# Splitting each expert weight piece into its high and low part with one instruction per engine instead of two

## The chip, the cores and the metric

The kernel runs on one core of a Trainium2 chip. The metric is the device time of one execution in microseconds (us). Engines are named as in the profile: PE is TensorE's matmul, PEld its weight load, DVE is VectorE, ACT is ScalarE, POOL is GpSimd, SP is the engine whose queue issues the weight DMAs. L174 is line 174 of the kernel before; the change adds three lines above the experts' code and one at its head, so L1209 before is L1213 after.

## The reference

Two layers of a decoder trunk over 256 tokens with model width 1024, all in float32. Each layer is a mixer (gated DeltaNet, convolution and attention heads between one input and one output projection) and a feed-forward part, each with a residual and a layer norm. The feed-forward part of layer 0 is dense; that of layer 1, which the change is about, sends each token to 2 of 8 experts of hidden width 3584:

```python
FFN_EXPERT = 7 * D_MODEL // 2          # 3584
logits = jnp.einsum('nd,de->ne', xf, w_router).astype(jnp.float32)
top_logits, top_idx = lax.top_k(logits, TOP_K)      # 2 of 8
gates = jax.nn.softmax(top_logits, axis=-1)
...
def expert_block(args):
    xb, e = args
    h = jax.nn.silu(xb @ w1[e]) * (xb @ w3[e])
    return h @ w2[e]
```

w1 and w3 are 1024 x 3584 and w2 is 3584 x 1024 for each expert. Every expert has tokens, so all 8 x 3 matrices are read, 352 MB.

## The kernel before

**Split products.** A float32 operand is split into a high part (type fp32r) and the low rest, and a product is the sum of three matmuls: high x high, high x low, low x high. `mm3` (L211) writes them: first, for each term, the two that use the weights' high part, and at the end of the group those that use the low part. `split` (L173) makes the two parts with one instruction each: ACT copies to the high part (L174), DVE subtracts it from the source (L175), so DVE's instruction waits for ACT's.

**A weight piece** is 128 partitions x 2048 columns of float32, 1 MB. `stage` (L177) issues its DMA on SP's queue into a tile `w`; `parts` (L189) allocates a tile `whi` and a tile `wlo` and splits the piece; `load` (L208) is the one after the other. Tiles come from two pools in turn, with 3 `w`, 2 `whi` and 2 `wlo` in each, so 6, 4 and 4 in all. `parts` splits in two halves of 128x1024, so a piece costs two instructions on ACT and two on DVE:

```python
        d = 2 if w.shape[1] == 2 else 1
        h = w.shape[d] // 2
        for c in (slice(0, h), slice(h, 2 * h)):
            c = (slice(None),) * d + (c,)
            split(w[c], *[t[c] for t in r])
        return r
```

A piece of w1 or w3 is cut by row blocks of the contraction (the first four of eight blocks, or the first two of four), a piece of w2 (two row blocks of 1024 columns) by columns, so that its first half feeds the output's columns 0 to 511 and the second half the columns 512 to 1023.

**The experts** (`moe`, L962) run after the router. Experts are ranked by their token count. `one_by_one` (L1195) takes four of them, each with up to 128 tokens, in 7 steps of 512 hidden columns: two pieces of w1, two of w3 (`first`, L1175), then the hidden tile h (Silu on ACT, L1208, product on DVE, L1209), then two pieces of w2 for the step before (`second`, L1184), then h is transposed on PE (L1218) and split into hT. That is 4 x 7 x 6 = 168 pieces. `side_by_side` (L1229) takes the largest expert, with up to 256 tokens, together with the three smallest of up to 64, in 14 steps of 256 hidden columns and a closing step: each step has one piece each of w1, w3 and w2 for the large one (matmuls at L215 to L224, hidden tile L1248 and L1249) and for each of the three small ones, whose matmuls are packed (`mm_packed`, L1164, matmuls at L1168 to L1172). That is another 14 x 12 = 168 pieces. `gather` (L1088) brings an expert's tokens together beforehand, `scatter` (L1127) adds its result to the residual; both come in small steps between the others. A branch for overfull experts (L1371) holds more pieces and is not executed with these inputs. The names in the rows: whi, wlo and w are a piece's tiles, x the gathered tokens, t a PSUM tile of the first layer, py one of the second layer, hT and jT the transposed hidden tile of a small and of the large expert.

**The order on each engine** is not written by hand: the framework's scheduler simulates a timeline (L1415) and issues each engine's instructions in the order that comes out. On PE it places the first matmul on a piece of w2 ahead of other work where that matmul's half is ready, and the rest of the piece later.

Of the kernel before, what the change touches and what calls it, by code (L numbers as in the profile page):

```python
# [38 lines left out]
def tile_hybrid_decoder(ctx: ExitStack, tc: tile.TileContext, x_in, w_in, mix_scale, w_out, gdn_conv_w,  # L39
# [7 lines left out]
    mixers = ctx.enter_context(ExitStack())  # L47
    mcst = mixers.enter_context(tc.tile_pool(name="mcst", bufs=1, reuse_waits="tile"))

    wp = {"more": None, "small": None, "n": 0,  # L50
          "base": ctx.enter_context(tc.tile_pool(name="wgt", bufs=1, side="right", reuse_waits="tile"))}


# [80 lines left out]
    par, small = [], []  # L134
# [38 lines left out]
    def split(src, hi, lo):  # L173
        S.activation(hi, src, AF.Copy)  # L174
        return V.tensor_sub(lo, src, hi.bitcast(F32))  # L175
# [13 lines left out]
    def parts(staged):  # L189

        which, w = staged
        r = []
        m = w.shape[1] * w.shape[2]
        for name, n in (("whi", WB[1]), ("wlo", WB[2])):
            if wp["small"] and m <= 1024:
                t = wp["small"].tile([128, 1024], F32R, name=name, tag=name, bufs=1)
            else:
                t = wp[which].tile([128, 2048], F32R, name=name, tag=name, bufs=n)
            r.append(t[:, :m].rearrange("p (a b) -> p a b", a=w.shape[1]))

        d = 2 if w.shape[1] == 2 else 1
        h = w.shape[d] // 2
# [5 lines that stand above are left out]
    def load(*args):  # L208
        return parts(stage(*args))
# [52 lines left out]
    def layer_norm_block(b, y, gam, bet, lp):  # L262

        xb = xt[:, b, :]
        r = lp.tile([128, D], F32, name="lnr", tag="lnr", bufs=2) if y else xb
        for h, yy in enumerate(y or ()):
            V.scalar_tensor_tensor(r[:, 512 * h:512 * h + 512], xb[:, 512 * h:512 * h + 512], ALPHA, yy,
                                   op0=OP.mult, op1=OP.add)
        st = lp.tile([128, 2, 6], F32, name="lnst", tag="lnst", bufs=2)
        for h in range(2):  # L270
            V.bn_stats(st[:, h, :], r[:, 512 * h:512 * h + 512])  # L271
        mv = lp.tile([128, 2], F32, name="lnmv", tag="lnmv", bufs=2)
        V.bn_aggr(mv, st)  # L273
        rs = lp.tile([128, 1], F32, name="lnrs", tag="lnrs", bufs=2)
        rsqrt_small(rs, mv[:, 1:2], 1, LN_EPS, 1.0, lp)
        for h in range(2):
            c = slice(512 * h, 512 * h + 512)
            V.scalar_tensor_tensor(r[:, c], r[:, c], mv[:, 0:1], gam[:, c], op0=OP.subtract, op1=OP.mult)  # L278
            last = V.scalar_tensor_tensor(xb[:, c], r[:, c], rs, bet[:, c], op0=OP.mult, op1=OP.add)  # L279
        return last  # L280
# [680 lines left out]

    def moe(l):  # L962
        li = l // 2
        with ExitStack() as es:
            gp = es.enter_context(tc.tile_pool(name="moe", bufs=1, reuse_waits="tile"))
            ps = es.enter_context(tc.tile_pool(name="eps", bufs=1, space=PSUM, reuse_waits="tile"))
# [41 lines left out]
            spare = [spare[0][:, :2048], spare[0][:, 2048:], gp.tile([128, 2048], F32, name="spare", tag="xg", bufs=2)]  # L1008
            early = [stage(*s, which=("more", "base")[i // 2]) for i, s in enumerate(piece_list[:4])]
            early[:2] = [parts(s) for s in early[:2]]  # L1010
            early += [stage(*s) for s in piece_list[4:10]]
            early += [stage(*s, into=t) for s, t in zip(piece_list[10:], spare)]

            def fetch(*src):
                nonlocal early
                if not early:
                    return load(*src)
                w = early.pop(0)
                return w if isinstance(w, list) else parts(w)
# [356 lines left out]
            n = None  # L1376
            for b in range(NB):
                with tc.issue_after(n.ins) if n else nullcontext():
                    n = layer_norm_block(b, None, gam, bta, gp)
# [8 lines left out]
    mixer(1)  # L1388
    mixers.close()
    moe(1)  # L1390


# [26 lines left out]
```

## Time and profile before

| | |
|---|---|
| median of 3 runs | 1656.45 us |
| lowest and highest | 1655.86 and 1656.79 us |
| the profiled execution | 1652.18 us |
| its span on the core | 1650.0 us |
| granted TensorE clock, mean | 0.983 |

The span is what the trace covers; the profiled execution is 2.18 us longer than its span, and 4.27 us shorter than the median of the runs. The experts' pieces are worked on from about 590 to about 1623 us; what is before are the first layer and the second mixer, what is behind is the last scatter and layer norm.

### The profile page before, as it was taken

What the parts mean: (1) busy time and instruction counts of PE and PEld (TensorE: products, weight loads), DVE (VectorE), ACT (ScalarE), POOL (GpSimd) and SP (SyncE); (2) the same over time, 40 slices, a digit from 0 to 9 for tenths busy, and PEclk for the clock granted to TensorE, in tenths of its full rate; (3) what the DMA queues carried; (4) which work ended last, traced back from release to release, by engine and by line L of the source; (5) the groups of instructions that cost most, each with busy time, mean ns of one, the idle gap of its engine ahead of it and who ended that gap; (6) DMA issues with size and microseconds to landing.
All of it is one profiled execution on the core that took longest, in us unless ns stands there. A gap on an engine that the chain in (4) does not pass through costs nothing. (4 is left out here: it accounts for less than half of the span.)

```text
span 1650.0 us, 28322 instructions
## 1 busy us (share of the span) xinstructions
PE 1573.9 (95%) x11218; PEld 1365.8 (83%) x11218; DVE 1369.6 (83%) x1902; ACT 1020.6 (62%) x1375; POOL 66.3 (4%) x82
## 2 busy tenths in 40 slices
PE   7999999999899989999999999999999999999995
PEld 6887799997888768888888888888988889888893
DVE  7987854555998798998988889887998988899997
ACT  5234544442425557777777677676887776777782
POOL 5001100000201100000000000000000000000000
PEclk9998999999999999999999999999999999999998
DMA  5351755532324577999999999998999989999991
GB/s 153 98 167 50 245 195 191 177 115 79 91 65 155 189 255 267 360 367 340 359 345 347 330 345 352 344 330 273 359 363 332 347 305 333 366 318 340 342 375 62
DMA packets 274796, 430.05 MB, mean 261 GB/s; under 512 B 11900, under 2 KB 181938, under 8 KB 274656
## 3 DMA queue, kind: packets, MB, share of 16 engines
q1 hardware_dynamic: 272864, 423.81, 74.8%
q0 software_dynamic: 1792, 4.35, 0.8%
q8 instruction: 90, 1.47, 0.4%
q14 instruction: 50, 0.41, 0.1%
HBM read 427.08 MB, written 1.05 MB: 259 GB/s over the span
## 5 line engine op out<-in xcount | busy, mean ns | idle before, releaser
L175 DVE TENSOR_TENSOR wlo<-w,whi 128x1024 fp32r<-128x1024 f32 (+1 forms) x812 | 939.1, 1204 | 135.2 <-ACT whi L174 127.5
L174 ACT ACTIVATE whi<-w 128x1024 fp32r<-128x1024 f32 (+1 forms) x812 | 792.1, 1037 | 231.3 <-PE py L217 43.3
L215 PE MATMUL t<-whi,x 128*128 128x512 f32 x448 | 179.4, 401 | 0.5 <-DVE x L175 0.5
L217 PE MATMUL t<-whi,x 128*128 128x512 f32 x448 | 176.1, 393 | 0.0
L222 PE MATMUL t<-wlo,x 128*128 128x512 f32 x448 | 124.5, 396 | 0.0
L215 PE MATMUL t<-x,whi 128*128 128x256 f32 x448 | 109.5, 282 | 0.0
L219 PE MATMUL t<-x,whi 128*128 128x256 f32 x448 | 109.4, 282 | 0.0
L215 PE MATMUL pj<-xth,whi 128*128 128x256 f32 x368 | 99.3, 303 | 6.6 <-ACT whi L174 2.5
L215 PEld LDWEIGHTS t<-whi,x 128*128 128x128 f32 x448 | 84.3, 188 | 20.1 <-DVE x L175 0.7
L222 PEld LDWEIGHTS t<-wlo,x 128*128 128x128 f32 x448 | 83.8, 188 | 20.1 <-DVE wlo L175 0.4
L217 PEld LDWEIGHTS t<-whi,x 128*128 128x128 f32 x448 | 84.4, 188 | 18.2
L219 PE MATMUL pj<-xtl,whi 128*128 128x256 f32 x368 | 95.7, 294 | 0.0
L1168 PE MATMUL t<-whi,x 128*128 128x256 f32 x588 | 86.9, 287 | 8.5 <-DVE x L175 3.3
L1170 PE MATMUL t<-wlo,x 128*64 128x256 f32 x672 | 93.8, 281 | 0.0
L1168 PEld LDWEIGHTS t<-whi,x 128*128 128x128 f32 x588 | 77.8, 190 | 14.6 <-DVE h L1249 4.4
L215 PE MATMUL py<-whi,hT 128*128 128x512 f32 x224 | 88.0, 393 | 0.0
L217 PE MATMUL py<-whi,hT 128*128 128x512 f32 x224 | 87.4, 390 | 0.0
L219 PE MATMUL ph<-xtl,whi 128*128 128x256 f32 x352 | 85.4, 281 | 0.4 <-DVE xtl L260 0.4
L215 PE MATMUL ph<-xth,whi 128*128 128x256 f32 x352 | 85.3, 281 | 0.0
L219 PEld LDWEIGHTS t<-x,whi 128*128 128x128 f32 x448 | 84.4, 188 | 0.8
L215 PEld LDWEIGHTS t<-x,whi 128*128 128x128 f32 x448 | 84.4, 188 | 0.8
L1170 PEld LDWEIGHTS t<-wlo,x 128*64 128x64 f32 x672 | 81.1, 135 | 1.8
(430 smaller groups left out, 2814.9 us busy)
## 6 DMA issues: line engine op xcount, KB each, us to landing
w<-in_moe_w_dram SPq DMA_DIRECT2D x333, 1024.0 KB, 6.2
w<-in_ffn_w_dram SPq DMA_DIRECT2D x33, 1024.0 KB, 5.5
w<-in_w_in_dram SPq DMA_DIRECT2D x18, 1024.0 KB, 5.6
w<-in_w_out_dram SPq DMA_DIRECT2D x8, 1024.0 KB, 5.0
w<-in_w_in_dram SPq DMA_DIRECT2D x14, 512.0 KB, 4.3
spare<-in_moe_w_dram SPq DMA_DIRECT2D x3, 1024.0 KB, 7.8
xt<-in_x_dram SPq DMA_DIRECT2D x2, 512.0 KB, 4.0
gam<-in_ln_mix_g_dram POOLq DMA_DIRECT2D x2, 512.0 KB, 3.9
```

What stands on the lines that cost most here:

```text
L174: S.activation(hi, src, AF.Copy)
L175: return V.tensor_sub(lo, src, hi.bitcast(F32))
L215: T.matmul(o, a[0], b[0], start=first and i == 0, stop=False)
L217: T.matmul(o, a[1], b[0], start=False, stop=False)
L219: T.matmul(o, a[0], b[1], start=False, stop=False)
L222: m = T.matmul(o, a[0], b[1], start=False, stop=last and i == n - 1)
L1168: T.matmul(o, flat(a), b[0], start=first and i == 0, stop=False)
L1170: T.matmul(o[:64], a[:, 0, :], b[1], start=False, stop=False)
```

## The change

A flag `whole` is false at first and set at the head of `moe`. With it, `parts` splits a piece with one ACT instruction and one DVE instruction of 128x2048. Tiles, DMAs and matmuls are those of before, and all code ahead of `moe` is as it was.

```diff
-    wp = {"more": None, "small": None, "n": 0,
+    wp = {"more": None, "small": None, "n": 0, "whole": False,
           "base": ctx.enter_context(tc.tile_pool(name="wgt", bufs=1, side="right", reuse_waits="tile"))}
...
             r.append(t[:, :m].rearrange("p (a b) -> p a b", a=w.shape[1]))
+        if wp["whole"]:
+            split(w, *r)
+            return r
 
         d = 2 if w.shape[1] == 2 else 1
...
     def moe(l):
         li = l // 2
+        wp["whole"] = True
```

The scheduler orders the program anew. The order on SP and on POOL is the same as before. On PE the number of matmuls is the same; ACT and DVE have one instruction less for each piece.

On ACT, at the first hidden tile of `one_by_one` (h is the Silu, hT the split of its transpose), before:

```order
331 L174 ACTIVATE whi<-w 128x1024 x4
332 L1208 ACT_TABLE_LOAD
333 L1208 ACTIVATE h<-t_6960 128x512
334 L174 ACTIVATE whi<-w 128x1024 x4
335 L174 ACTIVATE hT<-t_7013 128x512
```

and with the change:

```order
331 L174 ACTIVATE whi<-w 128x2048 x2
332 L1212 ACT_TABLE_LOAD
333 L1212 ACTIVATE h<-t_6952 128x512
334 L174 ACTIVATE whi<-w 128x2048 x2
335 L174 ACTIVATE hT<-t_7005 128x512
```

Four pairs of halves have become four whole copies, in the same places between the other instructions.

On DVE at the same place (by, posj and oh belong to the router's and the gather's small work, h is the product that PE's first transpose reads), before:

```order
771 L175 TENSOR_TENSOR wlo<-w,whi 128x1024 x2
772 L1349 TENSOR_REDUCE posj<-by 128x8
773 L175 TENSOR_TENSOR wlo<-w,whi 128x1024 x2
774 L1348 TENSOR_TENSOR by<-job,gate 128x64
775 L1101 TENSOR_SCALAR oh<-slots,posj 128x128 x2
776 L1209 TENSOR_TENSOR h<-h,t_6985 128x512
777 L175 TENSOR_TENSOR wlo<-w,whi 128x1024 x2
```

and with the change:

```order
771 L175 TENSOR_TENSOR wlo<-w,whi 128x2048
772 L1353 TENSOR_REDUCE posj<-by 128x8
773 L175 TENSOR_TENSOR wlo<-w,whi 128x2048
774 L1352 TENSOR_TENSOR by<-job,gate 128x64
775 L1105 TENSOR_SCALAR oh<-slots,posj 128x128 x2
776 L1213 TENSOR_TENSOR h<-h,t_6977 128x512
777 L175 TENSOR_TENSOR wlo<-w,whi 128x2048
```

Each two halves have become one instruction; the sequence is otherwise the same.

On PE in `side_by_side`, where a small expert's w2 pieces meet the next first-layer pieces (py are outputs of the second layer, the numbered t tiles those of the first; in the trace the single matmul in the row ahead of the seven starts at 1498.92 us), before:

```order
5418 L1168 MATMUL py<-whi,hT 128x512
5419 L1170 MATMUL py<-wlo,hT 64x512 x2
5420 L1172 MATMUL py<-whi,hT 128x512
5421 L1168 MATMUL py<-whi,hT 128x512
5422 L1170 MATMUL py<-wlo,hT 64x512 x2
5423 L1172 MATMUL py<-whi,hT 128x512
5424 L1168 MATMUL py<-whi,hT 128x512
5425 L1168 MATMUL t_15026<-whi,x 128x256 x7
5426 L1170 MATMUL t_15026<-wlo,x 64x256 x8
```

and with the change:

```order
5350 L1172 MATMUL py<-whi,hT 128x512
5351 L1174 MATMUL py<-wlo,hT 64x512 x2
5352 L1176 MATMUL py<-whi,hT 128x512
5353 L1172 MATMUL py<-whi,hT 128x512
5354 L1174 MATMUL py<-wlo,hT 64x512 x2
5355 L1176 MATMUL py<-whi,hT 128x512
5356 L1172 MATMUL py<-whi,hT 128x512 x2
5357 L1172 MATMUL t_14436<-whi,x 128x256 x7
5358 L1174 MATMUL t_14436<-wlo,x 64x256 x8
```

The matmul that begins a new piece of w2 ahead of the first-layer work stands in the same place; the one on the piece's other 512 columns, which came later, now stands beside it.

## Rows read from the trace of the kernel before

**Rows 1.** The page's first part: busy time, share of the span and number of instructions of each engine, over the whole program.

```profile
PE 1573.9 (95%) x11218; PEld 1365.8 (83%) x11218; DVE 1369.6 (83%) x1902; ACT 1020.6 (62%) x1375; POOL 66.3 (4%) x82
```

**Rows 2.** Busy time by stretch: the whole 425 us of one_by_one that are clear of its beginning, and 525 us of side_by_side. Columns: the stretch, its length, busy time and number of instructions of PE, PEld, DVE, ACT and POOL, granted TensorE clock, DMA share, GB/s.

```profile
650.00:1075.00 425.00, 425.00 (x1916) 346.68 (x1915) 375.61 (x369) 313.41 (x355) 0.00 (x0) 1.00 0.97 350
1075.00:1600.00 525.00, 510.17 (x3506) 455.10 (x3505) 464.94 (x495) 393.62 (x481) 1.10 (x2) 0.99 0.99 336
```

**Rows 3.** Waits of PE's weight load (PEld), 650 to 1075 us (the same question for the matmuls themselves, PE, has no row in this stretch). Columns: engine, tile and line, what it waited for, us in total, times, longest.

```profile
PEld t L222 <- DVE wlo L175: 0.4, 1, 0.4
```

**Rows 4.** Waits of the matmuls (PE), 1075 to 1600 us, all rows of the answer; columns as before.

```profile
PE t L1168 <- DVE x L175: 3.3, 2, 2.9
PE t L1168 <- DVE h L1249: 3.1, 7, 0.6
PE py L1168 <- ACT whi L174: 2.9, 7, 1.3
PE t L1168 <- DVE xt L1143: 1.9, 2, 0.9
PE py L215 <- ACT whi L174: 1.7, 2, 1.4
PE py L1141 <- DVE yT L175: 1.2, 1, 1.2
PE py L1170 <- DVE wlo L175: 0.4, 2, 0.2
```

**Rows 5.** Waits of the weight load (PEld), 1075 to 1600 us, the rows of weight pieces; a tile py is an output of the second layer, filled from a piece of w2.

```profile
PEld py L1168 <- ACT whi L174: 5.7, 7, 1.8
...
PEld py L215 <- ACT whi L174: 3.3, 5, 1.8
PEld t L1275 <- DVE wlo L175: 3.2, 9, 0.4
```

**Rows 6.** Groups by line and shape: operation, tile out<-in, shapes, number, busy us, mean ns of one, idle time before them. The 128x1024 rows are the halves of full pieces, the 128x512 rows the halves of the input projection's smaller pieces.

```profile
L175 DVE TENSOR_TENSOR wlo<-w,whi 128x1024 fp32r<-128x1024 f32 x784 | 921.1, 1223 | 132.2 <-ACT whi L174 124.6 <-PE t L224 5.4 <-PE pj L224 1.4
L174 ACT ACTIVATE whi<-w 128x1024 fp32r<-128x1024 f32 x784 | 776.1, 1052 | 201.2 <-PE py L217 43.3 <-PE t L217 40.1 <-PE t L219 24.3
...
L175 DVE TENSOR_TENSOR wlo<-w,whi 128x512 fp32r<-128x512 f32 x28 | 18.4, 682 | 3.0 <-ACT whi L174 3.0
...
L174 ACT ACTIVATE whi<-w 128x512 fp32r<-128x512 f32 x28 | 16.1, 622 | 30.1 <-PE pj L219 18.2 <-DMA w<-in_w_in_dram 11.7
```

**Rows 7.** Timeline in one_by_one. Columns: start us, duration of the run of like instructions, engine, line, operation, tiles, shapes, number in the run, and in brackets the idle time before it and what ended it. ACT and DVE are here on the pieces to come; PE stands at the first matmul on two neighbouring pieces.

```profile
806.21 2.01 ACT L174 ACTIVATE whi<-w 128x1024 fp32r<-128x1024 f32 x2 [1.18 <-PE py L217]
...
807.30 2.36 DVE L175 TENSOR_TENSOR wlo<-w,whi 128x1024 fp32r<-128x1024 f32 x2 [0.40 <-ACT whi L174]
...
814.48 2.01 ACT L174 ACTIVATE whi<-w 128x1024 fp32r<-128x1024 f32 x2 [0.79 <-PE t L217]
...
815.44 0.39 PE L215 MATMUL t<-whi,x 128*128 128x512 f32 x1
...
818.23 0.39 PE L215 MATMUL t<-whi,x 128*128 128x512 f32 x1
```

**Rows 8.** Timeline at the start of one_by_one: the first hidden tile of the first job (h, line 1209) and its transpose on PE.

```profile
609.06 3.89 ACT L174 ACTIVATE whi<-w 128x1024 fp32r<-128x1024 f32 x4
...
610.16 2.35 DVE L175 TENSOR_TENSOR wlo<-w,whi 128x1024 fp32r<-128x1024 f32 x2
...
612.95 0.68 DVE L1209 TENSOR_TENSOR h<-h,t 128x512 f32<-128x512 f32 x1
...
613.78 0.63 PE L1218 MATMUL t<-ident,h 128*128 128x128 f32 x4 [2.08 <-DVE h L1209]
```

**Rows 9.** Timeline at three places in side_by_side: ACT's copy of a piece of w2, and PE's first matmul on it.

```profile
1241.06 2.00 ACT L174 ACTIVATE whi<-w 128x1024 fp32r<-128x1024 f32 x2
1242.16 0.50 PE L215 MATMUL py<-whi,jT 128*128 128x512 f32 x1 [0.27 <-ACT whi L174]
...
1315.16 1.99 ACT L174 ACTIVATE whi<-w 128x1024 fp32r<-128x1024 f32 x2
1316.25 0.50 PE L215 MATMUL py<-whi,jT 128*128 128x512 f32 x1 [1.38 <-ACT whi L174]
...
1497.82 2.94 ACT L174 ACTIVATE whi<-w 128x1024 fp32r<-128x1024 f32 x3
1498.92 0.50 PE L1168 MATMUL py<-whi,hT 128*128 128x512 f32 x1 [1.35 <-ACT whi L174]
```

**Rows 10.** ACT's timeline before the first and the second of these places.

```profile
1238.12 2.01 ACT L174 ACTIVATE whi<-w 128x1024 fp32r<-128x1024 f32 x2 [0.34 <-PE t L1172]
...
1308.23 2.00 ACT L174 ACTIVATE whi<-w 128x1024 fp32r<-128x1024 f32 x2
1310.74 3.89 ACT L174 ACTIVATE whi<-w 128x1024 fp32r<-128x1024 f32 x4
```

**Rows 11.** Busy time by stretch around two of PE's stalls, columns as in the second group; the thirteenth number is the granted clock.

```profile
1312.00:1316.30 4.30, 1.76 (x10) 0.96 (x8) 4.30 (x6) 4.28 (x6) 0.00 (x0) 1.00 1.10 354
1316.30:1320.00 3.70, 3.70 (x10) 2.87 (x11) 3.70 (x5) 1.76 (x3) 0.00 (x0) 0.56 1.03 381
...
1121.90:1125.70 3.80, 3.79 (x19) 3.79 (x20) 0.00 (x0) 1.04 (x2) 0.00 (x0) 0.55 0.81 260
```

**Rows 12.** Waits of the queue on SP that issues the weight DMAs, 650 to 1600 us.

```profile
SPq L186 <- DVE wlo L175: 665.4, 277, 8.7
```

## The prediction

> **What bounds the kernel now.** I read the shares of busy time first, then the experts' two stretches by engine, then who waits for whom there, and last single places in the timeline. Over the whole program PE is busy 95% of the span, DVE 83%, ACT 62% [rows 1]. The change touches the experts alone, so the stretches decide. In one_by_one PE is busy 425.00 of 425.00 us while DVE is at 375.61 (88%) and ACT at 313.41 (74%) [rows 2]; no matmul waits there for anything, and the weight load waits once, for 0.4 us [rows 3]. In side_by_side PE is busy 510.17 of 525 us [rows 2], and its waits add up to 14.5 us, all of them for ACT or DVE [rows 4]. So PE bounds the first stretch outright, and in the second PE with a few stalls. DVE is the next busiest engine, and the DMA queue is behind it: SP waits for DVE to free a weight tile, 665.4 us in 277 waits [rows 12]. The question is thus not how much work ACT and DVE shed, but whether a piece's parts reach PE earlier or later.
>
> **What it sheds.** 336 executed pieces lose one ACT and one DVE instruction each. No row has a 128x2048 split, so I extend the two shapes that there are. DVE takes 1223 ns for 128x1024 and 682 for 128x512 [rows 6]: 541 ns for each 512 columns, so 1223 + 2 x 541 = 2305 ns as an estimate. Two halves in a run take 2.36 us [rows 7], because back-to-back instructions overlap a little. So DVE sheds about 0.06 us a piece, 20 us in all. ACT by the same steps: 1052 + 2 x 430 = 1912 ns against 2.00 to 2.01 for a pair [rows 7, 9]: 0.1 us a piece, 33 us in all. Of these 53 us the path gets only what shortens one of PE's waits, since PE never stands for ACT or DVE in one_by_one.
>
> **What it delays.** PE may begin on a piece once the high part is written that it reads. Before, that was the first half, 1.05 us after ACT began; now it is the whole, after 1.91 us: +0.86 us. DVE's subtraction begins after ACT's copy, so the low part starts up to 0.86 us later too, though it ends at nearly the same time as the second half did. Where does PE come that soon after ACT?
>
> *one_by_one: at nothing.* ACT begins a piece when PE leaves a high tile (at 814.48 us, when the last L217 on an earlier piece is through [rows 7]). With four such tiles, three pieces then lie ahead of it, and PE begins a new one every 2.8 us (815.44, 818.23 [rows 7]): some 8 us of cover against 0.86. Without it, 168 pieces would cost up to 168 x 0.86 = 144 us, but the one wait of 0.4 us [rows 3] says that the cover is there.
>
> *The start of one_by_one: +0.75 us.* PE's transpose waits 2.08 us for h; ahead of h DVE does two halves from 610.16, behind the ACT copy that began at 609.06 [rows 8]. The order keeps this sequence, with one whole in the place of the two. Its ACT copy now ends at about 609.06 + 1.91 = 610.97, so DVE begins some 0.8 us later and needs 0.06 less: h and the transpose move by 0.75.
>
> *side_by_side: +7 us.* Here the scheduler put the first matmul on a piece of w2 right behind its half: ACT begins at 1241.06, 1315.16 and 1497.82, PE's matmul starts 1.09 to 1.10 us later, after 0.27, 1.38 and 1.35 us of waiting [rows 9]. The order on PE after the change has these matmuls in the same places. The weight load shows 7 + 5 = 12 such waits for a high part [rows 5]. If ACT began each copy when it does now, 12 x 0.86 = 10.3 us would be added; with 2 us for low parts (9 waits that are already there, 3.2 us in all [rows 5]) 12.3. ACT also gains: where it works back to back through the pieces ahead it arrives 0.1 us earlier for each. Before the stop at 1315.16 three pieces stand without a wait on ACT, before that at 1241.06 one, behind a wait of 0.34 for PE that takes back what was won earlier [rows 10]. Taking half of the 12 places with one piece (0.75 us late) and half with four (0.45) gives 6 x 0.75 + 6 x 0.45 = 7.2, and I take 7. The low end is that a later PE frees tiles later, or stands at the next wait for less, so that a delay is absorbed: 0. The high end is 12.3.
>
> *What the shedding gives back: -2.5 us.* The 12 waits for DVE's h, xt, yT and x are 9.5 us [rows 4]. Ten of them (h, xt and yT) have about three whole pieces on DVE ahead: 10 x 3 x 0.06 = 1.8; the other two, for x (3.3 us, at the change from one stretch to the next), get an order of their own, which I put at -0.7. Bounds: from 0 to 4.5, a little under half of the waits.
>
> **The Trainium skill on this.** Rows first: PE stands for ACT's copy 4.6 us in nine waits in side_by_side, and ACT is at 75% there [rows 2, 4]. The Trainium skill ("Perfetto Trace Analysis", Optimizing Scalar/DVE Operations) says that larger operations help if the engine is saturated; "If Scalar/Vector aren't saturated, but are causing bubbles on other engines, breaking up instructions may allow work to be completed sooner." By that sentence alone halves are right here and nothing would be given back: +7.75 us, 1664.2. The trace agrees in so far as it shows these bubbles; I still count the 2.5 us, because 14 of PE's 23 waits are for DVE, which is at 89% [rows 2, 4].
>
> **Sum.** 0.75 + 7 - 2.5 = +5.25 us, taken as +5, against the profiled execution's 1652.2: 1657.2. That execution is 4.3 us below the median of the runs shown, so on the median it is 1656.45 + 5 = **1661.5 us**, or 0.3% slower. About 0.2% (3.3 us) is what a measurement of this kernel can tell from no change, so the forecast is slower by little more than that.
>
> **Rivals.**
>
> *No difference that can be told (0.34).* The delays are absorbed: each late matmul in side_by_side stands ahead of work that has a wait of its own for DVE (14 of PE's 23 waits are for DVE [rows 4]), and the new order is free to differ where the clock of the simulation moves. For it speaks that one_by_one has nothing to lose, and that all of PE's stalls make 14.5 us, so a change of a fifth in them vanishes. Against it: the stops are on ACT, ACT's copy alone got longer, and PE's order is the same there. Time: 1653.2 to 1659.7, about 1657.
>
> *Faster (0.16).* DVE sets the pace, not PE: at 88 and 89% [rows 2] it would only take small stops between its instructions to fill it, and every weight tile is freed by it [rows 12]. It decides if weight tiles, not PE's matmuls, are what ends last. Then the 336 x 0.06 = 20 us that it sheds come off: 1636; if that holds only in side_by_side, 168 x 0.06 = 10 us: 1646. For it speaks the share; against it that PE had no wait at all in 425 us. The Trainium skill ("Perfetto Trace Analysis", Identifying the Most-Contended Engine) counts PE by its weight loads, since matmul busy time is no measure; by weight loads PE has 346.68 of 425 us and DVE's 375.61 would be the bound. The trace disagrees in one_by_one: what DVE makes lies there some pieces ahead of PE.
>
> *Slower by more (part of the 0.50).* All 12.3 + 0.75 us of lateness arrive, and the stalls grow long enough for the clock. After the stall that ends at 1316.25 [rows 9] the granted clock is 0.56 over 3.7 us, after that of 1121.9 0.55 over 3.8 [rows 11], the lower level of 1.2 GHz; with PE half idle from 1312.0 to 1316.3 (1.76 busy of 4.30) that came behind. Each such stretch costs about 3.7 x 0.45 = 1.7 us. Two more give 3.4: +16, or 1672.
>
> That the change doesn't do what it says is out: the order shows one 128x2048 instruction in the place of each two.
>
> **Chances and range.** Slower by over 0.2%: 0.50, which is my sum and the case above; within 0.2%: 0.34; faster by over 0.2%: 0.16, mostly 1646 to 1653. The range goes from 1652 (no delay arrives and all 4.5 us are given back) to 1672; what is left out is the case of DVE as the bound.
>
> **What would show it.** Right: splits of 128x2048 at 2.25 to 2.35 us on DVE and 1.9 on ACT, DVE's busy time down by some 20 us and ACT's by some 33; one_by_one still without a wait on PE and as long as before; PE's waits on whi in side_by_side up from 4.6 us to some 10; the start's wait for h up from 2.08 to about 2.8. Wrong: one_by_one shorter or longer by over 2 us (then the split does set the pace or the cover is thinner than I read), side_by_side's waits on whi unchanged, or splits of 2048 columns that take much more or less than the two halves.

## The result and the profile after

The change is slower: 1676.48 us against 1656.15, a ratio of 1.0123 with an interval of 1.0096 to 1.015. The direction was forecast, the size was not: +20 us instead of +5, and the time lies above the range's end of 1672. A second set of runs (r1_after_again below) gave 1677.92 against 1652.7 us on its chip, 1.016 (1.0145 to 1.0176). The profiled execution of the change took 1679.53 us, with a span of 1677.8; the second profile has 1675.26. Two of the six runs of f3_side_not_n0 and one of the twelve of h2_quarters_not_close took 8601 us, none of any other kernel did, and why is open; the times and ratios below are of the other runs.

The page's first part, which answers to [rows 1]:

```profile
PE 1581.1 (94%) x11218; PEld 1368.6 (82%) x11218; DVE 1346.7 (80%) x1566; ACT 992.9 (59%) x1039; POOL 66.3 (4%) x82
```

The two stretches, which answer to [rows 2] (the columns are those):

```profile
650.00:1075.00 425.00, 424.01 (x1904) 345.00 (x1903) 366.11 (x228) 299.66 (x213) 0.00 (x0) 1.00 0.97 347
1075.00:1600.00 525.00, 499.19 (x3391) 441.74 (x3390) 439.39 (x316) 371.90 (x304) 0.00 (x0) 0.99 0.96 325
```

DVE has shed 22.9 us and ACT 27.7, PE's busy time is up by 7.2. In one_by_one PE is busy in all but 1 us, which three waits for a low part make (650 to 1075 us; none before [rows 3]):

```profile
PE t L225 <- DVE wlo L175: 1.0, 3, 0.7
```

In the same 525 us of side_by_side, however, PE's busy time has fallen from 510.17 to 499.19: here it stands more than before. The split's two rows, against [rows 6]:

```profile
L175 DVE TENSOR_TENSOR wlo<-w,whi 128x2048 fp32r<-128x2048 f32 x333 | 753.9, 2285 | 129.7 <-ACT whi L174 121.6 <-PE t L227 7.9
L174 ACT ACTIVATE whi<-w 128x2048 fp32r<-128x2048 f32 x333 | 628.9, 1913 | 161.7 <-PE t L220 45.1 <-PE t L1176 28.1 <-PE py L220 26.5
```

2285 and 1913 ns, against estimates of 2305 and 1912. What the engines shed came about as forecast. PE's longest waits, 1075 to 1650 us, against [rows 4]:

```profile
PE t L1172 <- DVE h L1253: 10.0, 9, 1.3
PE t L1279 <- DVE both L1315: 5.5, 1, 5.5
PE py L1172 <- ACT whi L174: 4.1, 7, 1.5
PE py L218 <- ACT whi L174: 3.6, 5, 1.1
PE py L1118 <- ACT xs L1113: 2.6, 1, 2.6
PE t L1172 <- DVE xt L1147: 2.1, 3, 0.9
PE py L1174 <- DVE wlo L175: 1.7, 1, 1.7
PE py L1145 <- DVE yT L175: 1.5, 1, 1.5
```

The waits for h (L1253, before L1249) have gone from 3.1 us to 10.0, nine of them now and up to 1.3 us each; a wait of 5.5 us for `both` (the small experts' hidden tile, L1315) is new; the waits for the high part of a w2 piece are up from 4.6 to 7.7. The two waits for x (3.3 us) are gone, and one of 2.6 us for xs, a tile of the gather, is new.

To see where the time is lost I took each matmul of PE by its place in the program, and its start after minus its start before. The medians by stretch (us; the stretches are times of the kernel before), with the kernels of the next section beside it, all from the profiled executions:

| kernel | before the experts, 560:580 | after the first h, 630:650 | end of one_by_one, 1000:1100 | end of side_by_side, 1600:1617 | last scatter, 1625:1640 |
|---|---|---|---|---|---|
| the change | 0.5 | 5.6 | 7.4 | 23.2 | 27.8 |
| r1_after_again | -1.0 | 1.4 | 3.3 | 18.8 | 23.5 |
| e1_one_only | -0.7 | 0.3 | 2.2 | 1.4 | 1.7 |
| e2_side_only | 1.6 | 1.6 | 1.5 | 17.7 | 22.2 |
| e3_act_halves | 1.3 | 2.6 | 2.8 | 21.9 | 25.9 |
| e6_dve_halves | 2.1 | 3.5 | 3.5 | 23.5 | 29.0 |
| f1_side_w2 | 4.6 | 6.2 | 6.1 | 22.2 | 26.2 |
| f2_side_w13 | 0.7 | 0.7 | 0.7 | 5.8 | 10.8 |
| f3_side_not_n0 | 2.5 | 2.6 | 2.6 | 12.9 | 15.8 |
| f4_side_not_close | 2.7 | 5.4 | 5.4 | 24.7 | 27.6 |
| f5_n0_only | 3.4 | 3.4 | 3.3 | 8.1 | 11.8 |
| g1_w2_quarters | -0.7 | -0.6 | -0.6 | -3.2 | 1.2 |
| h2_quarters_not_close | 1.3 | 1.3 | 1.3 | -1.3 | -2.6 |

The first column is code that no kernel changes, and it moves by up to 5.6 us: that much of a single profile is chance, so the steps from column to column are to be read. They hold chance too: f4's row is of an execution of 1679.21 us, where the median of its runs is 1672.25. For the change, in its two profiles: 5.1 and 2.4 us to the first h, 1.8 and 1.9 in one_by_one, 15.8 and 15.5 in side_by_side, 4.6 and 4.7 at its end.

**The wait for h.** In each step of side_by_side PE needs a PSUM tile whose reader is DVE's product h. One such place, the kernel before (timeline, columns as in [rows 7]):

```profile
1256.71 2.01 ACT L174 ACTIVATE whi<-w 128x1024 fp32r<-128x1024 f32 x2 [0.87 <-PE t L219]
...
1257.81 2.36 DVE L175 TENSOR_TENSOR wlo<-w,whi 128x1024 fp32r<-128x1024 f32 x2 [0.65 <-ACT whi L174]
...
1260.08 0.42 DVE L1249 TENSOR_TENSOR h<-h,t 128x256 f32<-128x256 f32 x1
...
1260.56 0.63 PE L1168 MATMUL t<-whi,x 128*128 128x256 f32 x3 [0.55 <-DVE h L1249]
```

and the same place after the change:

```profile
1265.67 1.92 ACT L174 ACTIVATE whi<-w 128x2048 fp32r<-128x2048 f32 x1 [0.96 <-PE t L222]
...
1267.62 2.29 DVE L175 TENSOR_TENSOR wlo<-w,whi 128x2048 fp32r<-128x2048 f32 x1 [1.57 <-ACT whi L174]
...
1269.83 0.41 DVE L1253 TENSOR_TENSOR h<-h,t 128x256 f32<-128x256 f32 x1
...
1270.30 0.87 PE L1172 MATMUL t<-whi,x 128*128 128x256 f32 x5 [1.33 <-DVE h L1253]
```

ACT is not held up: it begins at 1265.67 as soon as PE has left the tile. DVE begins 1.95 us behind ACT instead of 1.10, because it needs all of the high part, and the whole subtraction ends 4.2 us behind ACT's start instead of 3.5. h is queued behind it on DVE, and PE's next first-layer matmul behind h: 1.33 us of waiting for 0.55. The new order has little part in this: by DVE's timeline 23 of the 28 h of side_by_side have as many pieces straight ahead of them as before. The five others include the two places where a wait is new (0.24 and 1.33 us); there two pieces stand ahead of h instead of one.

**The start.** The same at the first h, against [rows 8]:

```profile
612.51 3.76 ACT L174 ACTIVATE whi<-w 128x2048 fp32r<-128x2048 f32 x2
...
614.46 2.29 DVE L175 TENSOR_TENSOR wlo<-w,whi 128x2048 fp32r<-128x2048 f32 x1 [0.96 <-ACT whi L174]
...
617.19 0.68 DVE L1213 TENSOR_TENSOR h<-h,t 128x512 f32<-128x512 f32 x1
...
618.02 1.09 PE L1222 MATMUL t<-ident,h 128*128 128x128 f32 x4 [2.77 <-DVE h L1213]
```

The wait is 2.77 for 2.08, +0.7 as worked out beforehand (0.75). e1_one_only below has the same wait, and in its profile this place is 0.7 us later and nothing more.

**The end.** In the last step of side_by_side the scheduler has put things into another order. Before:

```profile
1613.84 2.35 DVE L175 TENSOR_TENSOR wlo<-w,whi 128x1024 fp32r<-128x1024 f32 x2
...
1613.95 0.85 ACT L1310 ACTIVATE both<-both 64x768 f32<-64x768 f32 x1 [0.88 <-DVE both L1294]
...
1616.12 0.94 DVE L1311 TENSOR_TENSOR both<-both 64x768 f32<-64x768 f32 x1
...
1617.55 0.58 PE L1275 MATMUL t<-ident,both 64*128 64x64 f32 x6
```

and after:

```profile
1639.62 2.27 DVE L175 TENSOR_TENSOR wlo<-w,whi 128x2048 fp32r<-128x2048 f32 x1
...
1641.82 0.67 DVE L175 TENSOR_TENSOR yT<-py,yT 128x512 fp32r<-128x512 f32 x1
1642.27 0.83 ACT L1314 ACTIVATE both<-both 64x768 f32<-64x768 f32 x1
1642.42 2.27 DVE L175 TENSOR_TENSOR wlo<-w,whi 128x2048 fp32r<-128x2048 f32 x1
1644.62 0.67 DVE L175 TENSOR_TENSOR yT<-py,yT 128x512 fp32r<-128x512 f32 x1
1645.22 0.94 DVE L1315 TENSOR_TENSOR both<-both 64x768 f32<-64x768 f32 x1
...
1646.30 0.87 PE L1279 MATMUL t<-ident,both 64*128 64x64 f32 x6 [5.48 <-DVE both L1315]
```

Before, one piece stood between the last sum for `both` and DVE's product, and PE went on at 1617.55 without a wait. Now two yT (for the scatter) and two whole splits stand on DVE in front of the product, and ACT's Silu is late as well; PE waits 5.48 us. The kernel before had a wait of 1.4 us for yT behind this place, which is gone; the end as a whole is 4.6 us later.

### The profile page after: what moved, and what is told of

Read it like the earlier page. It is cut to its first block, busy times and chain, and to the rows that moved or that the text cites. A ratio compares the mean times of both kernels' runs of the same rounds, so it can differ in the third digit from the quotient of the medians.

```text
span 1677.8 us, 27655 instructions
## 1 busy us (share of the span) xinstructions
PE 1581.1 (94%) x11218; PEld 1368.6 (82%) x11218; DVE 1346.7 (80%) x1566; ACT 992.9 (59%) x1039; POOL 66.3 (4%) x82
## 5 line engine op out<-in xcount | busy, mean ns | idle before, releaser
L175 DVE TENSOR_TENSOR wlo<-w,whi 128x2048 fp32r<-128x2048 f32 (+2 forms) x479 | 916.1, 1938 | 183.4 <-ACT whi L174 173.5
L174 ACT ACTIVATE whi<-w 128x2048 fp32r<-128x2048 f32 (+2 forms) x479 | 763.0, 1627 | 255.5 <-PE t L220 45.1
L218 PEld LDWEIGHTS pj<-xth,whi 128*128 128x128 f32 x368 | 73.8, 200 | 10.3 <-ACT whi L174 3.1
```

The source lines that it names most:

```text
L218: T.matmul(o, a[0], b[0], start=first and i == 0, stop=False)
```

## Experiments

Theory A: inside a piece the two engines no longer overlap (DVE begins 0.86 us later, and so does the first matmul on the piece), and this is paid where PE has no lead, at h and at the w2 pieces of side_by_side. Rival B: it is the length of the instructions; whatever is queued behind one waits longer. Rival C: it is the scheduler's new order. All ratios are to the kernel before on the same chip.

### Which stage: e1_one_only, e2_side_only

The edits in this section are shortened, and words in brackets are notes.

```diff
     (e1, ahead of side_by_side's first load)
+    wp["whole"] = False
     (e2: not at moe's head, but ahead of side_by_side's first load)
-        wp["whole"] = True
+                wp["whole"] = True
```

> Whole pieces in one_by_one alone, halves in side_by_side. Theory A (the hand-over between ACT and DVE inside a piece is lost: DVE begins 0.86 us later, so does the first matmul on the piece; it costs only where PE has no lead): one_by_one has its lead, so only the start pays, 2 to 4 us over the kernel before; side_by_side's waits on h stay at 0.55 to 0.6 us each. Rival C (the scheduler's new order is what costs, above all the stall of 5.5 us at the end of side_by_side): also near the kernel before, as the end is in halves.

Measured: 1654.91 against 1652.99 us, 1.0013 (1.0001 to 1.0025).

> Halves in one_by_one, whole pieces in side_by_side alone. Theory A: nearly all of the change's 20 us come back, 15 to 20 us over the kernel before, with waits on h of 1.33 us and with the late first matmuls on w2 pieces. Rival C: 4 to 6 us if the stall at the end is what costs, and nothing if that stall is not in this order.

Measured: 1673.59 against 1652.99 us, 1.0137 (1.0113 to 1.0162). So +2 and +20.6 us, just under and just over what A said: one_by_one's cover holds but for little, and side_by_side has nearly all of the loss. C alone would have made 4 to 6.

### Which half of the split: e3_act_halves, e6_dve_halves

```diff
+        if wp["whole"]:                      (e3)
+            for c in halves: S.activation(hi[c], w[c], AF.Copy)
+            V.tensor_sub(lo, w, hi.bitcast(F32))
+        if wp["whole"]:                      (e6)
+            S.activation(hi, w, AF.Copy)
+            for c in halves: V.tensor_sub(lo[c], w[c], hi[c].bitcast(F32))
```

> ACT copies two halves, DVE subtracts the whole piece in one. Theory A: the high part of the first half is there as early as before, so the first matmuls on w2 pieces wait as before (4.6 us in all); but DVE must wait for both halves, begins 0.95 us later, and h stands behind it: waits on h of 1.3 to 1.4 us each, together 8 to 12 us over the kernel before. Rival B (it is the length of the instructions that other work queues behind, not the hand-over): the same waits on h, since DVE's instruction is long, so this run alone does not part the two.

Measured: 1677.87 against 1652.99 us, 1.0151 (1.0131 to 1.0171). PE's waits, 1075 to 1650 us:

```profile
PE t L1178 <- DVE h L1259: 13.2, 10, 4.0
...
PE py L1178 <- ACT whi L206: 2.8, 7, 0.9
...
PE py L224 <- ACT whi L206: 1.6, 2, 0.8
```

The high parts are early again (4.4 us of waits, before 4.6), but h is waited for 13.2 us, one time 4.0. The place was right, the size was not: +24.9 us instead of 8 to 12, and the time has no gain from the early high part. A part of the excess is the clock: in the steps of side_by_side this profile is at the lower level (granted clock 0.50) for 17.1 us in four stretches, the kernel before for 6.8 in two.

> ACT copies the whole piece in one, DVE subtracts two halves. Theory A: DVE begins 0.86 us later as in the change, although its instructions are short, and the first matmul too: waits on h of 1.3 to 1.4 us, 15 to 22 us over the kernel before, as in the change. Rival B: short DVE instructions let h through as before, waits on h of 0.55 to 0.6 us, and only the late first matmuls remain, 5 to 8 us.

Measured: 1684.33 against 1652.99 us, 1.0189 (1.0163 to 1.0214), worse than either theory said. PE's waits, 1075 to 1650 us:

```profile
PE t L1178 <- DVE h L1259: 12.7, 9, 1.4
```

With short DVE instructions h is waited for 1.40 to 1.42 us each time, 12.7 in all, where B said 0.55 to 0.6. That refutes B in this form: a short DVE instruction is not enough, DVE has to begin early, which takes a short instruction on ACT; and by e3 a short one on ACT is not enough either. Only halves on both let the two engines overlap.

### Which pieces: f5_n0_only, f3_side_not_n0, f2_side_w13, f1_side_w2

The piece that stands ahead of h on DVE is, by DVE's order, the first of the three w2 pieces for the small experts in each step, one of twelve. The expectations call it that of the first small expert; in fact the small experts come one after another, and the three pieces of a step are three consecutive blocks of 256 hidden columns, mostly of one expert, and not one of each as the description of the kernel has it.

```diff
     (f5; f3 sets i > 0, and True behind the load)
+                            wp["whole"] = i == 0
                             hi, lo = load(jb.rows(moe_w2)[:, 2 * fs:2 * fs + 2, :], 2, D)
+                            wp["whole"] = False
     (f2, in side_by_side alone; f1 with == 2)
-        if wp["whole"]:
+        if wp["whole"] and w.shape[1] != 2:
```

> Halves everywhere except the w2 piece of the first small expert in each step of side_by_side: 14 whole pieces of 336. Theory A: the waits on h are 1.33 us as in the change, 6 to 7 us, and this piece's first matmul up to 0.8 us late in some steps: 6 to 9 us over the kernel before. Rival B: 14 of 168 pieces, so 1 to 2 us, not to be told from no change.

Measured: 1660.97 against 1653.43 us, 1.0056 (1.0035 to 1.0077): +7.5 us from 14 whole pieces of 336, inside A's 6 to 9. PE's waits, 1075 to 1650 us:

```profile
PE t L1171 <- DVE h L1252: 9.7, 10, 1.4
...
PE t L1278 <- DVE both L1316: 1.8, 1, 1.8
```

The waits for h are up by 6.6 us, as A said, but only five of the ten are 1.33 us or longer. By the table side_by_side's steps cost 4.8 us (this profile has no stretch at the lower clock after 1316, which is 1.7 less) and the end 3.7, of which A had nothing.

> Whole pieces in side_by_side except the w2 piece of the first small expert, one of 12 in a step; one_by_one in halves. Theory A: the waits on h go back from 1.33 to 0.55 us (6 to 7 us), that piece's own first matmul too (1 to 2 us), and the end has its old order (5 us): 7 to 10 us over the kernel before, against 20.6 with all pieces of side_by_side whole. Rival B: 14 pieces of 168 give back a twelfth, so 18 to 19 us, or 14 with the end.

Measured: 1667.40 against 1653.43 us, 1.0087 (1.0072 to 1.0101). PE's waits, 1075 to 1650 us:

```profile
PE t L1171 <- DVE h L1253: 5.2, 9, 0.8
...
PE t L1279 <- DVE both L1317: 2.2, 1, 2.2
```

The waits for h went from 12.4 us (e2) to 5.2, and the end from 5.6 to 2.2. By the table side_by_side's steps cost 10.3 us for e2's 16.2, the 6 that A said, and the end 2.9 for 4.5, where A had 5 less. By the medians it is +14, outside A's 7 to 10, and the figure that B gave with the end; but B's way there, a twelfth off the steps and the whole end, is not what the table shows. A is right on h and wants a further price for the other whole pieces: the waits for high parts are 8.4 us here, before 4.6. The order at the end is not quite the old one (see f4).

> Whole pieces in side_by_side for w1 and w3 alone; its w2 pieces and one_by_one in halves. Theory A (hand-over lost, paid at two kinds of places: the matmul that begins a w2 piece right behind its first half, and h, which on DVE stands behind one w2 piece of the first small expert in each step): neither place has a whole piece, so waits on h of 0.55 to 0.6 us as before and first matmuls as before; only the end keeps its new order (the small experts' product both behind two yT on DVE), 4 to 6 us over the kernel before. Rival B (whatever other work queues behind long instructions): most of the 20 us remain, since 8 or 9 of 12 pieces in a step are whole.

Measured: 1664.25 against 1653.43 us, 1.0076 (1.0058 to 1.0094): +10.8, between A and B. PE's waits, 1075 to 1650 us:

```profile
PE t L1171 <- DVE h L1253: 5.9, 9, 1.5
PE t L1279 <- DVE both L1315: 5.9, 1, 5.9
```

By the table 5.0 us are the end, as A said, and 5.1 side_by_side's steps, for which A had nothing. Eight of the nine waits for h are back at 0.54 to 0.57 us, but there are nine for the seven of before and one is 1.55; that is 2.8 us more in all, and the rest of the 5 I could not place.

> Whole pieces in side_by_side for w2 alone (56 pieces of 336). Theory A: h's waits at 1.33 us (7 us), the first matmuls on w2 pieces late as in the change (5 to 6 us), the end in the new order (4 to 5 us): 15 to 19 us over the kernel before, nearly all that whole pieces in the whole of side_by_side cost. Rival B: a third of the pieces, a third of the loss, 6 to 8 us.

Measured: 1671.77 against 1652.7 us, 1.0123 (1.0104 to 1.0142): +19, at A's upper end; a third of the pieces costs nearly as much as all of them. B's 6 to 8 is out. f1 and f2 together make 30 us and e2 20.6; both contain the late end (by the table 4.0 and 5.0 us), which is half of the excess.

### The end: f4_side_not_close

```diff
                 for f in range(n + 1):
+                    wp["whole"] = f < n - 1
```

> Whole pieces in side_by_side except its last two steps; one_by_one in halves. The order on DVE at the end is that of before (both ahead of yT). Theory A with C as one of its parts: the stall of 5.5 us and its stretch at the lower clock are gone, 14 to 16 us over the kernel before. If that stall only moves (the end is late whatever the order), 20 us as with all pieces of side_by_side whole.

Measured: 1672.25 against 1653.43 us, 1.0114 (1.0099 to 1.0129), +18.8: nearer to "only moves". By the table the end costs 2.9 us for e2's 4.5, and PE's wait for `both` is 1.9 us. But the order is not that of before: the product is ahead of both yT again, yet two pieces stand ahead of it where the kernel before has one:

```profile
1638.56 4.62 DVE L175 TENSOR_TENSOR wlo<-w,whi 128x1024 fp32r<-128x1024 f32 x4
...
1643.10 0.94 DVE L1316 TENSOR_TENSOR both<-both 64x768 f32<-64x768 f32 x1
```

f3 and f5 have two pieces there as well. e1 and h2, whose order there is that of before, lose nothing to speak of at the end (+0.3 and -1.3). So no run has whole pieces with the old order, and whether the 3 to 5 us of the end are C's alone is open. In the steps before the end the new order can account for the two new waits for h, 1.6 us of the change's 15 to 16.

### Once more, and the other way: r1_after_again, g1_w2_quarters, h2_quarters_not_close

> The change once more, for a second profile. All theories: 16 to 24 us over the kernel before. If the three stretches at the lower clock between 586 and 622 us, which only the first profile of the change and one experiment show, come with a run and not with the change, this profile can be without them and about 5 us shorter, with side_by_side as long as in the first.

Measured: 1.016 (above). In the first profile of the change the granted clock is 0.72 on the mean from 586 to 592 us, from 596 to 602 and from 616 to 622, the last one behind the wait for h; in the second it is 0.79, 1.00 and, behind h, 0.72. So the stretch at 596 came with the run. The one behind h did too, though both profiles have it. e1_one_only has the change's wait for h and no such stretch, and f4_side_not_close has halves there, a wait of 2.06 us, and has it (columns as in [rows 2]; the rows are e1's wait, then the clock in the first profile, the second, e1 and f4):

```profile
614.09 0.63 PE L1222 MATMUL t<-ident,h 128*128 128x128 f32 x4 [2.75 <-DVE h L1213]
...
616.00:622.00 6.00, 3.98 (x14) 3.40 (x15) 5.81 (x14) 1.00 (x3) 0.00 (x0) 0.72 1.01 356
...
612.00:618.00 6.00, 4.15 (x15) 3.51 (x16) 5.63 (x14) 0.99 (x3) 0.00 (x0) 0.72 0.98 333
...
612.00:618.00 6.00, 3.91 (x19) 3.33 (x20) 5.83 (x14) 2.33 (x3) 0.00 (x0) 1.00 1.02 353
...
616.00:622.00 6.00, 4.39 (x15) 3.61 (x16) 5.46 (x15) 1.69 (x3) 0.00 (x0) 0.72 1.03 373
```

```diff
     (g1, in side_by_side alone)
+        if wp["whole"] and w.shape[1] == 2:
+            for c in (row block k, columns 512 * hf to 512 * hf + 512) for hf, k in (0, 0), (0, 1), (1, 0), (1, 1):
+                split(w[c], *[t[c] for t in r])
+            return r
     (h2, beside it)
                 for f in range(n + 1):
+                    wp["whole"] = f < n - 2
```

> The opposite of the change where theory A says that it hurts: w2 pieces of side_by_side in four quarters of 128x512, all others in halves. The first matmul on such a piece needs one quarter, 0.62 instead of 1.05 us after ACT begins, and DVE can begin 0.43 us earlier. Theory A: first matmuls wait less (4.6 us of waits go to 1 to 2), waits on h a little less: 2 to 6 us faster than the kernel before. Rival: the 112 added instructions on each engine (0.1 us on ACT and 0.12 us on DVE for each two) fill DVE, which is at 89%: 0 to 5 us slower.

Measured: 1655.08 against 1652.7 us, 1.0018 (1.0009 to 1.0027): slower by 2.4 us. A's 2 to 6 faster missed, and the rival's 0 to 5 slower has the number. Yet the table has it 2.6 us ahead at the end of side_by_side's steps (1.7 of it the stretch at the lower clock after 1316 [rows 11], which this profile has not), and PE's waits for h are 3.2 us, before 3.1, so the added instructions do not fill DVE; it loses 4.4 at the end. There (timeline):

```profile
1617.85 2.48 DVE L175 TENSOR_TENSOR wlo<-w,whi 128x512 fp32r<-128x512 f32 x4
...
1620.25 0.55 DVE L175 TENSOR_TENSOR hT<-t,hT 128x384 fp32r<-128x384 f32 x1
...
1620.85 0.79 PE L1177 MATMUL py<-whi,hT 128*128 128x512 f32 x1 [2.38 <-DVE hT L175]
```

hT, split for the last small pieces, stands behind four quarters that the scheduler has put ahead of it, and PE waits 2.38 us. The stretch at the lower clock there lasts 6.8 us instead of the 3.4 of the kernel before, some 1 us more of PE's time.

> As g1 (w2 pieces of side_by_side in quarters), but the last three of its steps in halves, where the order at the end is that of before. Theory A: g1 was 3.2 to 3.9 us ahead of the kernel before in the middle of side_by_side and lost 4 at the end, where hT stood behind four quarters on DVE; without that loss 2 to 4 us faster than the kernel before. Rival: the lead of g1's one profile is a stretch at the lower clock fewer (1.7 us) and chance; 0 to 2 us faster, not to be told from no change.

Measured: 1649.53 against 1653.49 us, **0.998 (0.9968 to 0.9992)**, 3 to 4 us faster than the kernel before, and the fastest kernel of this study. PE's waits, 1075 to 1650 us:

```profile
PE t L1177 <- DVE h L1259: 3.0, 6, 0.6
PE py L1177 <- ACT whi L174: 2.3, 4, 1.4
...
PE py L224 <- ACT whi L174: 1.3, 2, 1.0
```

The waits for the high part of w2 pieces are 3.6 us for 4.6, those for h 3.0 for 3.1. By the table this profile gains 3.9 us from the first column to the last, and two stretches at the lower clock that the profile of the kernel before has are not in it, after 1316 [rows 11] and after 1620; the matmuls behind them start 1.6 and 1.3 us sooner. Over all runs it is less: span times what the granted clock lacks of 1, an estimate of the most that the lower level can cost, is 27.3 us on the mean of its eleven runs and 29.3 for the kernel before on that chip, 2 us of the gain. So the result is faster, but the rival is not excluded as to the cause: the shorter waits themselves are worth 1 to 2 us.

## Why the prediction was too small

**What was right.** PE bounds one_by_one and its cover holds but for three places, where PE waits for a low part: +1.9 us there in the second profile, just within the 2 that would have shown it wrong, and e1 is +2. The start's term (+0.75) measured +0.7. What the engines shed (20 and 33 us) measured 22.9 and 27.7, and nothing of it can be seen on the path. The first matmuls on w2 pieces were worth +3.1 us of PE's waits (4.6 to 7.7) and 4.8 of the weight load's (9.0 [rows 5] to 13.8) against 7.2: the right mechanism, rather too large.

**The step that failed** is "what the shedding gives back: -2.5 us", and under it the reading that the low part "ends at nearly the same time as the second half did". In the place shown DVE's pair ended 3.5 us behind ACT's start, and the whole ends 4.2 behind it: 0.8 later, and so is all that is queued behind. I counted the ten waits on h, xt and yT as shortened by what three pieces on DVE save, 1.8 us. They were lengthened from 6.2 to 13.6 us, +7.4, nearly all of it h, from 3.1 to 10.0. The working for the start has the very mechanism (DVE's whole split begins 0.8 us later, h is behind it, PE behind h), and I used it in that one place, because a DVE that is busy 89% of the stretch looked like a queue that never stands. It does stand: in the place shown it was idle 0.65 us before the split, until ACT's copy, and 1.57 after, and one piece stands between that and h, not three. f5 has only the 14 pieces ahead of h whole and is 7.5 us longer; its row of the table puts 4.8 in the steps and 3.7 at the end. The term's other part, -0.7 for x, came out (3.3 us of waits gone, 2.6 for xs new), but it was a guess, so this is luck.

**What the sum had no term for** is the end: the orders ahead of the prediction are of three other places. The new order and the late splits cost 4.6 us in the profile: a new wait of 5.5 us for `both`, one of 1.4 for yT gone, and some 1 us more at the lower clock (PE works at it for 5.4 us instead of 3.4). How much of it goes back with the old order is open (f4).

**The rivals.** DVE as the bound is refuted: in f5, f2 and the change it has less to do and PE waits more; h2 gives it 92 instructions more and is faster. The weight DMAs, whose engines are busy 97 and 99% of the two stretches [rows 2], are not the bound either: between 650 and 1600 us ACT's copies never wait for one in the kernel before, and once, for 1.5 us, in the change. The Trainium skill ("Perfetto Trace Analysis", Optimizing Scalar/DVE Operations), cited for the change's loss, has the direction right for joined instructions in side_by_side: 1.0137 (e2). On breaking up further the runs are divided: 1.0018 with quarters in every step (g1), 0.998 where the last steps are left out (h2), and there the clock has a part. "No difference" fell with e2: delays were not absorbed, since a late h stalls PE in step after step. The clock's part was forecast in kind. By the estimate used for h2 the lower level costs the kernel before 28.1 us on the mean of its sixteen runs beside r1, and r1 36.2 on the mean of five, so about 8 of the 25 us; the first four runs of the change have 32.2. Which stall brings a stretch is not settled by its length: a wait of 1.7 us for a low part at about 1470 has one behind it in both profiles of the change, but in e2 the granted clock is 1.00 from 1470 to 1476, behind the same wait. The stretch at 1316 is in both kernels, but not in f5, g1 or h2.

In sum, by the second profile: the start 2.4 (0.3 before the experts, 0.7 of wait for h, 1.3 at the lower clock behind it; the stretch at the lower clock at 589 is made up for by a wait for sel, a tile of the router, of 0.2 instead of 1.7), one_by_one 1.9, side_by_side 15.5, the end 4.7. In side_by_side's steps PE's waits are 26.8 us instead of 14.5: h 6.9 more, high parts 3.1, the late low part 1.3, `both` 1.2, xt and yT 0.5, x and xs 0.7 less. With 1.7 us more at the lower clock that is 14.0, and 1.5 are not placed.

## What to carry to other kernels

Two engines that work on one piece in turn overlap only as far as the piece is cut: joining two instructions saves little (here 0.07 us a piece on DVE and 0.09 on ACT), but delays the second engine by about half of the first one's (here 0.85 of 1.91 us). Look for what is queued behind the second engine (here h, one instruction of 0.4 us), not only for who reads the piece; work out a mechanism once and then look for every place in the order where it holds. Do not cut coarse where a consumer stands at the first part; where the lead is pieces long the coarse cut gained nothing here either (e1, +2 us). Look at the last step by itself: its order can change, and there is little behind it to cover a wait.

## What was not expected of the hardware

Which waits are followed by a stretch at the lower clock (1.2 GHz) changes from one execution to the next: between 586 and 622 us the same program had three such stretches in one profile and two in the other, and was 4.2 us apart at the first h, 1.5 of which had come before the experts. A stretch behind the first h came with the change's wait of 2.8 us in two profiles and not in that of e1, and with the old wait of 2.1 in that of f4 and not in that of the kernel before. By the table's first column, code that is the same instruction for instruction ends up to 5.6 us apart.
